# RWKV head sums and norm means as two fp32r passes, with three reorderings around the state chain

## The chip, the cores and the metric

The kernel runs on one core of a Trainium2 chip. The metric is the device time of one execution in microseconds. Five engines share the work: TensorE (PE; its weight loads are shown as PEld), VectorE (DVE), ScalarE (ACT), GpSimd (POOL) and SyncE (SP), which issues the DMAs. All matrix products write to PSUM, from where DVE or ACT take them back.

## The reference, cut to what matters

One decoder layer takes 512 prompt tokens and 8 sequences of 4 sample tokens (544 columns in the kernel, 32 of them samples). It has two branches, an mLSTM and an RWKV-7 branch, which share one input projection, then an output projection and an MLP. The change lies in the RWKV branch alone, which has 16 heads of 64 channels:

```python
kkh = kkh / jnp.maximum(jnp.linalg.norm(kkh, axis=-1, keepdims=True), 1e-12)   # sum over a head
sa = jnp.einsum('bhvk,bhk->bhv', S, -kk)
S = S * w[:, :, None, :] + sa[..., None] * (kk * a)[:, :, None, :] + v[..., None] * k[:, :, None, :]
o = jnp.einsum('bhvk,bhk->bhv', S, r)                                          # token by token
o = head_norm(o, RWKV_NORM_EPS) * lnx_w + lnx_b                                # mean and variance per head
o = o + (rh * kh * r_k).sum(-1, keepdims=True) * vh                            # another head sum
```

## The kernel before

**Layout.** Channels stand on the 128 partitions, tokens along the free axis. Two heads of 64 channels share the partitions, so the RWKV branch is eight "pairs" p = 0 to 7. The 512 prompt tokens are cut in 8 chunks of 64; within a chunk the token recurrence is solved by products, and only the state goes from chunk to chunk.

**Products.** The large projections are done in `mm3` (lines 311 to 316): each fp32 operand is split in a high and a low part of type fp32r, and three fp32r products (L314, L315, L316) replace one fp32 product. A projection of 128 channels is 48 such products (8 blocks of rows, two halves of the columns, three each). The small products of the RWKV branch are plain fp32. In the trace an fp32 product stands as two instructions, an fp32r product as one, and a transpose as one.

**One pair.** `g_proj` (L604) projects k, r and v. `g_prep` (L628) forms the decays and the scaled operands: `heads_sum` (L559) adds the squares of k over each head with the block matrix `bones` (first call at L651), products of `ar` and `bk` (L707) give the masked matrices `g1` and `gk`; `g1` goes through DRAM to be inverted. L750 transposes the `a` half of `ar` by 16 products with the identity into `za` (copied at L751). L756 is the second head sum. L779 transposes v into `sv` (four copies at L783), and L789 multiplies `g1` with it on 64 rows at a time. `g_inv` (L792) solves blocks of 16 rows on DVE (L802, L804), sends the result through DRAM, and completes the inverse by small products. `g_chain` (L855) applies the inverse (L867), forms the transition matrices (L880) and the state input (L889), and goes through the chunks: L899 multiplies the state with the transition matrix, L900 on DVE adds the chunk's input, and two output products per chunk stand in the same loop (L903). L907 adds the part of the output that comes from the state. Then come the head norm's two means, by `bmean` (L912, L919). `g_srows` (L1021) does the same norm for the sample rows (L1026, L1032).

**Order.** Each of these functions is a generator. What it yields is a due time; `merge` (L1041) takes the segment with the smallest base plus due time next, so a due time that has already passed means "at once". That fixes the order of the program. A list scheduler then lays out each engine's queue from the program order and its own estimate of when an operation is ready, so an engine's order can differ from the program's: the trace shows the chain's products between the projections of later pairs. Every queue is worked off in order. Tiles come from pools: `rp` has two buffers for each name, `r1` one, `tp` (PSUM) two, `big()` (PSUM) two.

Of the kernel before, what the change touches and what calls it, by code (L numbers as in the profile page):

```python
# [10 lines left out]
F32 = mybir.dt.float32  # L11
F32R = mybir.dt.float32r
AF = mybir.ActivationFunctionType
ALU = mybir.AluOpType
# [8 lines left out]
NS = NB * NT  # L23
T = NS + NP
# [17 lines left out]
def hybrid_kernel(ctx: ExitStack, tc: tile.TileContext, I, O):  # L42
    nc = tc.nc
    V = nc.vector
    S = nc.scalar
    G = nc.gpsimd
    PE = nc.tensor
# [4 lines left out]
    const = ctx.enter_context(tc.tile_pool(name="const", bufs=1))  # L52
# [12 lines left out]
    def tp(shape):  # L65
        return psB.tile(shape, F32, name="tp")


    ident = const.tile([128, 128], F32)
# [4 lines left out]
    G.memset(onesd, 1.0 / D)  # L74
    bones = const.tile([128, 128], F32)
    G.memset(bones, 0.0)
    G.memset(bones[0:64, 0:64], 1.0)
    G.memset(bones[64:128, 64:128], 1.0)
    bmean = const.tile([128, 128], F32)
    G.memset(bmean, 0.0)  # L80
    G.memset(bmean[0:64, 0:64], 1.0 / 64)
    G.memset(bmean[64:128, 64:128], 1.0 / 64)

# [169 lines left out]
    ps = tp([128, 8, 9])  # L253
# [5 lines left out]
    for k in range(8):  # L259
        ps = big()  # L260
# [5 lines left out]
    ps = tp([128, 128])  # L266
# [23 lines left out]
    nkk = const.tile([128, 8], F32)  # L290
# [242 lines left out]
    with tc.issue_after(mm.ins):  # L533
        ps = proj_w(*xsp, 0, 276, 276, ((0, 6), (6, 8)))
# [5 lines left out]
    r1 = pool(late, "r1", 1, "right")  # L540
# [17 lines left out]

    def heads_sum(mat, src):  # L559
        ps = big()  # L560
        for j, (a, n) in enumerate(HALF):
            PE.matmul(ps[:, j, 0:n], mat, src[:, a:a + n], start=True, stop=True)
        return ps
# [64 lines left out]
    def g_prep(p, s):  # L628
# [21 lines left out]
        S.activation(sq, k_, AF.Square, scale=kkc)  # L650
        ps = heads_sum(bones, sq)  # L651
        S.activation(lw, lw, AF.Copy, scale=CDEC, bias=CDEC)
# [32 lines left out]
        b3, m3 = c8(bp[:, NS:T]), c8(km[:, NS:T])  # L685
        ar = rp.tile([128, 8, 2, 64], F32, name="ar")
        V.scalar_tensor_tensor(ar[:, :, 0, :], k3, nkk[:, p:p + 1], wp[:, :, 0:64], op0=ALU.mult, op1=ALU.mult)
        V.tensor_tensor(ar[:, :, 1, :], r3, wp[:, :, 1:65], op=ALU.mult)
        bk = r1f.tile([128, 8, 3, 64], F32, name="bk")
# [11 lines left out]
        for i, c0 in enumerate((0, 4)):  # L701
            yield 14.83 + 3 * i
            cs = slice(c0, c0 + 4)
            pts = [tp([128, 4, 2, 64]) for h in range(2)]
            for j in range(4):
                for h, q in enumerate(halves):
                    PE.matmul(pts[h][:, j].rearrange("p a b -> p (a b)"),  # L707
                              bk[q, c0 + j, h:h + 2, :].rearrange("p a b -> p (a b)"),
                              ar[q, c0 + j].rearrange("p a b -> p (a b)"), start=True, stop=True)
# [36 lines left out]
        s["za"] = za  # L746
        pt = tp([128, 8, 64])
# [8 lines left out]
        ps = heads_sum(bones, bv)  # L756
        for h, q in enumerate(halves):
# [15 lines left out]

        sv = rp.tile([128, 8, 2, 64], F32, name="sv")
        s["sv"] = sv
        yield 16.44
        pt = tp([128, 4, 128])
        for i in range(4):
            PE.transpose(pt[:, i, :], v_[:, NS + 128 * i:NS + 128 * i + 128], ident)  # L779
        sve = sv.rearrange("p (a e) h v -> p a e h v", e=2)  # L780
        for e, q in enumerate(halves):
            for h in range(2):
                S.copy(sve[halves[1 - h], :, e, h, :], pt[q, :, 64 * h:64 * h + 64])  # L783
        yield 22.9
        pt = tp([128, 8, 64])
        for c in range(8):
            for h, q in enumerate(halves):
                o = halves[1 - h]
                PE.matmul(pt[q, c, :], g1[o, c, h, :], sv[o, c, h, :], start=True, stop=True)  # L789
        S.copy(za[:, :, 1, :], pt)  # L790
# [64 lines left out]
    def g_chain(p, s):  # L855
# [16 lines left out]
        for c0 in (0, 4):  # L872
            yield 59.2 + 0.2 * c0
            j0 = 1 if c0 == 0 else 0
            cs = slice(c0 + j0, c0 + 4)
            n = 4 - j0
            pt = tp([128, 4, 2, 64])
            for j in range(j0, 4):
                for h, q in enumerate(halves):
                    PE.matmul(flat(pt[q, j]), zz[q, c0 + j, :], flat(gk[q, c0 + j, h]), start=True, stop=True)  # L880
            for h, q in enumerate(halves):
                V.tensor_tensor(xmd[q, cs, 64 * h:64 * h + 64], pt[q, j0:4, 1, :],
                                ident[q, q].unsqueeze(1).to_broadcast([64, n, 64]), op=ALU.add)
            V.tensor_tensor(ar[:, cs, 1, :], ar[:, cs, 1, :], pt[:, j0:4, 0, :], op=ALU.add)
        yield 60.6
# [8 lines left out]
        po = psC.tile([128, 8, 64], F32, name="po")  # L894
        for c in range(8):
            yield 61.2 + 1.0 * c
            if c > 0:

                PE.matmul(pcn[:, c, :], xmd[:, c, :], st[:, c - 1, :], start=True, stop=True)  # L899
                V.scalar_tensor_tensor(sc[:, 0:64] if c == 7 else st[:, c, :], pcn[:, c, :], wend[:, c:c + 1],  # L900
                                       st[:, c, :], op0=ALU.mult, op1=ALU.add)
            for h, q in enumerate(halves):
                PE.matmul(po[q, c, :], sv[:, c, h, :], gk[:, c, h, 0, :], start=c == 0, stop=False)  # L903
        yield 68.3
        for c in range(1, 8):
            for h, q in enumerate(halves):
                PE.matmul(po[q, c, :], st[q, c - 1, :], ar[q, c, 1, :], start=False, stop=c == 7)  # L907
# [113 lines left out]
    def g_srows():  # L1021
# [3 lines left out]
        pm = tp([128, 8, NS])  # L1025
        PE.matmul(pm, bmean, o8, start=True, stop=True)  # L1026
        V.tensor_tensor(o8, o8, pm, op=ALU.subtract)
# [3 lines left out]
        pm = tp([128, 8, NS])  # L1031
        PE.matmul(pm, bmean, q8, start=True, stop=True)  # L1032
        S.activation(q8, pm, AF.Sqrt, bias=eps_b)
# [421 lines left out]
    for p in range(8):  # L1455
        st = {}
# [257 lines left out]
```

## Time and profile before

| what | value |
|---|---|
| median of three runs | 1423.55 us (1420.78 to 1434.56) |
| the profiled execution's own time | 1417.81 us |
| its span (first to last instruction) | 1416.1 us |
| PE / PEld / DVE / ACT / POOL busy | 96 / 85 / 59 / 43 / 5% of the span |
| mean granted TensorE clock | 0.985 |

The pairs' work lies between about 100 and 620 us. "Busy" for PE counts an instruction from its start to the end of its pipeline, and neighbouring products overlap, so the time that a product takes from the engine is read from the distance between two starts, not from its duration. A "granted clock" of 1.00 is the full 2.4 GHz and 0.50 is 1.2 GHz.

### The profile page before, as it was taken

The page shows a single profiled execution, that of the slowest core. Times are in us where ns is not written, and L with a number is a line of the kernel's source. Part 1 is how long each engine was busy: PE and PEld are TensorE (multiplying, and loading weights), DVE is VectorE, ACT ScalarE, POOL GpSimd, SP SyncE. Part 2 cuts the span into 40 slices and gives each one's busy share as a digit, 9 for nine tenths or more (in the row PEclk, how much of TensorE's full clock was granted, in tenths as well). Part 3 has the DMA queues.
Part 4 walks back from the last instruction along what each step waited for, and adds up shares of the span by engine and source line. Part 5 has one row for each costly group of instructions (what it writes and reads, how often), then busy time and mean ns, then how long its engine had stood idle before and what let it go on. Part 6 is the DMA issues. An engine that isn't in the chain of part 4 may idle for free.

```text
span 1416.1 us, 29923 instructions
## 1 busy us (share of the span) xinstructions
PE 1363.6 (96%) x12272; PEld 1202.5 (85%) x12272; DVE 831.9 (59%) x2002; ACT 608.0 (43%) x1133; POOL 70.9 (5%) x292
## 2 busy tenths in 40 slices
PE   6999999999999999999999999999999999999996
PEld 3878887888887878888888888678899999999996
DVE  3677575857667686566556465387943343443446
ACT  2465454545545455364454444533741231321320
POOL 6000000000000000011101010000000000000000
PEclk9999999999998999999999999999999999999999
DMA  9432222122222211253655744753513323333321
GB/s 281 126 68 53 67 50 54 46 60 54 60 56 49 69 43 38 57 146 105 204 159 154 243 128 139 237 182 119 149 61 90 90 75 92 88 90 90 103 77 64
DMA packets 251483, 145.66 MB, mean 103 GB/s; under 512 B 52683, under 2 KB 244413, under 8 KB 251323
## 3 DMA queue, kind: packets, MB, share of 16 engines
q1 hardware_dynamic: 251347, 143.75, 35.5%
q8 instruction: 97, 1.59, 0.5%
q14 instruction: 39, 0.32, 0.1%
HBM read 124.58 MB, written 19.14 MB: 101 GB/s over the span
## 4 chain that ended last, share of the span: by engine, by line
PE 77%; DVE 7%; ACT 6%; DMA 5%; issue 3%; SPq 1%; POOL 0%; POOLq 0%; DVEq 0%; ACTq 0%
PE mm L314 17%; PE mm L315 16%; PE mm L316 16%; PE tp L707 2%; DVE wlo L302 1%; DMA craw<-in_w_cond_dram 1%; ACT whi L300 1%; PE tp L340 1%; PE tp L1300 1%; PE pcn L899 1%; PE po L1317 1%; PE tp L880 1%; PE po L903 1%; DMA wraw<-in_w_up_dram 1%; PE tp L867 1%
## 5 line engine op out<-in xcount | busy, mean ns | idle before, releaser
L314 PE MATMUL mm<-hhi,whi 128*128 128x272 f32 (+1 forms) x1712 | 510.6, 299 | 4.1 <-ACT hhi L1529 1.3
L315 PE MATMUL mm<-hlo,whi 128*128 128x272 f32 (+1 forms) x1712 | 502.5, 294 | 0.9 <-DVE hlo L1530 0.8
L316 PE MATMUL mm<-hhi,wlo 128*128 128x272 f32 (+1 forms) x1712 | 500.3, 292 | 0.5 <-DVE wlo L302 0.5
L314 PEld LDWEIGHTS mm<-hhi,whi 128*128 128x128 f32 x1712 | 323.6, 189 | 20.2 <-issue 10.2
L315 PEld LDWEIGHTS mm<-hlo,whi 128*128 128x128 f32 x1712 | 323.6, 189 | 6.6 <-DVE hlo L1530 2.1
L316 PEld LDWEIGHTS mm<-hhi,wlo 128*128 128x128 f32 x1712 | 323.8, 189 | 5.5 <-issue 4.0
L300 ACT CAST whi<-wraw 128x1024 fp32r<-128x1024 f32 (+1 forms) x142 | 146.1, 1029 | 395.4 <-PE mm L315 382.7
L302 DVE TENSOR_TENSOR wlo<-wraw,whi 128x1024 fp32r<-128x1024 f32 (+1 forms) x142 | 170.0, 1198 | 140.0 <-ACT whi L300 137.4
L314 PE MATMUL mm<-hid,whi 128*128 128x272 f32 x384 | 110.8, 289 | 0.0
L316 PE MATMUL mm<-hid,wlo 128*128 128x272 f32 x384 | 110.7, 288 | 0.0
L315 PE MATMUL mm<-hil,whi 128*128 128x272 f32 x384 | 110.4, 288 | 0.0
L314 PEld LDWEIGHTS mm<-hid,whi 128*128 128x128 f32 x384 | 72.3, 188 | 0.5 <-ACT hid L1539 0.5
L315 PEld LDWEIGHTS mm<-hil,whi 128*128 128x128 f32 x384 | 72.3, 188 | 0.0
L316 PEld LDWEIGHTS mm<-hid,wlo 128*128 128x128 f32 x384 | 72.1, 188 | 0.0
L1414 DVE TENSOR_TENSOR g1s<-mm,mod 128x32 f32<-128x32 f32 x48 | 9.1, 190 | 102.3 <-PE mm L316 102.1
L1418 DVE SCALAR_TENSOR_TENSOR xt<-mm,mod,xt 128x240 f32<-128x240 f32 (+2 forms) x92 | 43.6, 476 | 9.3 <-PE mm L316 9.2
L1099 DVE SCALAR_TENSOR_TENSOR acc<-qr,chalf,acc 128x512 f32<-128x512 f32 (+1 forms) x96 | 43.5, 496 | 0.7 <-ACT acc L1097 0.2
L802 DVE TENSOR_TENSOR itmp<-xi,ai 128x2 f32<-128x2 f32 (+14 forms) x120 | 29.8, 248 | 15.4 <-POOL ai L722 12.3
L1539 ACT CAST hid<-rl 128x544 fp32r<-128x544 f32 (+1 forms) x37 | 21.6, 585 | 39.1 <-DVE rl L1538 39.1
L1540 DVE TENSOR_TENSOR hil<-rl,hid 128x544 fp32r<-128x544 f32 (+1 forms) x37 | 23.9, 647 | 19.4 <-ACT hid L1539 19.3
L707 PEld LDWEIGHTS tp<-ar,bk 64*128 64x128 f32 x256 | 25.8, 194 | 9.2 <-issue 6.8
L707 PE MATMUL tp<-ar,bk 64*128 64x128 f32 x256 | 33.1, 304 | 0.5 <-DVE gk L712 0.5
(553 smaller groups left out, 2199.7 us busy)
## 6 DMA issues: line engine op xcount, KB each, us to landing
wraw<-in_w_in_dram SPq DMA_DIRECT2D x66, 512.0 KB
craw<-in_w_cond_dram SPq DMA_DIRECT2D x48, 512.0 KB
wraw<-in_w_up_dram SPq DMA_DIRECT2D x32, 512.0 KB
wraw<-in_w_down_dram SPq DMA_DIRECT2D x32, 512.0 KB
cs<-in_state_mlstm_C_dram SPq DMA_DIRECT2D x32, 256.0 KB
out_C_s_dram<-cs SPq DMA_DIRECT2D x32, 256.0 KB
wraw<-in_w_out_dram SPq DMA_DIRECT2D x12, 384.0 KB
xp<-in_x_prompt_dram SPq DMA_DIRECT2D x2, 2048.0 KB
```

The source lines that it names most:

```text
L300: S.copy(hi, raw)
L302: V.tensor_tensor(lo, raw, hi.bitcast(F32), op=ALU.subtract)
L314: PE.matmul(out, hi[k], xhi[k], start=first and k == 0, stop=False)
L315: PE.matmul(out, hi[k], xlo[k], start=False, stop=False)
L316: PE.matmul(out, lo[k], xhi[k], start=False, stop=last and k == n - 1)
L340: mm = PE.matmul(ps[32 * g:32 * g + 32, i, :], cth[:, 4 * half + g, :], raws[ci][half][:, g, :], start=half == 0, stop=half == 1)
L707: PE.matmul(pts[h][:, j].rearrange("p a b -> p (a b)"), bk[q, c0 + j, h:h + 2, :].rearrange("p a b -> p (a b)"), ar[q, c0 + j].rearrange(" ...
L802: V.tensor_tensor(tmp[:, 0:nq, 0:t + 1], xi[:, 0:nq, 0:t + 1], ai[:, 0:t + 1, t].unsqueeze(1).to_broadcast([128, nq, t + 1]), op=ALU.mult)
L1099: V.scalar_tensor_tensor(a, qr[:, base + j * step:base + j * step + n], w(j), a, op0=ALU.mult, op1=ALU.add)
L1418: V.scalar_tensor_tensor(d, ps[:, o:n], mod[:, goff + m, 0:1], d, op0=ALU.mult, op1=ALU.add)
L1539: S.copy(hid[:, f, a:a + n], rl)
L1540: V.tensor_tensor(hil[:, f, a:a + n], rl, hid[:, f, a:a + n].bitcast(F32), op=ALU.subtract)
```

## The change

It does four things.

1. `bones` and `bmean` become fp32r. Every head sum and every mean is formed by splitting the source in a high part (a copy on ACT) and a low part (a subtraction on DVE), and by two fp32r products that add up in PSUM, in place of one fp32 product. The parts have one buffer each (`shi`, `slo` in `r1`).
2. `ar` is stored with the `a` half and the `r` half apart, and the `a` half is transposed in four 128 by 128 blocks, with four copies on ACT, in place of 16 products with the identity and one copy.
3. `sv` gets zeros in its unused quarters (two GpSimd memsets per pair), moves to a pool with one buffer, and L789 works on all 128 rows.
4. The 16 output products of L903 stand ahead of the chain over chunks, not in it. Two due times change (16.44 to 28, 22.9 to 33); both have passed when they are reached, as the old ones had.

```diff
-    bones = const.tile([128, 128], F32)
+    bones = const.tile([128, 128], F32R)
...
-    def heads_sum(mat, src):
+    def parts_of(src):
+        n = src.shape[1]
+        hi = r1.tile([128, T], F32R, name="shi")[:, 0:n]
+        S.copy(hi, src)
+        lo = r1.tile([128, T], F32R, name="slo")[:, 0:n]
+        V.tensor_tensor(lo, src, hi.bitcast(F32), op=ALU.subtract)
+        return hi, lo
+
+    def sum2(out, mat, hi, lo):
+        PE.matmul(out, mat, hi, start=True, stop=False)
+        PE.matmul(out, mat, lo, start=False, stop=True)
+
+    def heads_sum(src):
+        hi, lo = parts_of(src)
         ps = big()
         for j, (a, n) in enumerate(HALF):
-            PE.matmul(ps[:, j, 0:n], mat, src[:, a:a + n], start=True, stop=True)
+            sum2(ps[:, j, 0:n], bones, hi[:, a:a + n], lo[:, a:a + n])
...
-        ar = rp.tile([128, 8, 2, 64], F32, name="ar")
+        ar = rp.tile([128, 2, 8, 64], F32, name="ar")
...
-        for c in range(8):
-            for q in halves:
-                PE.matmul(pt[q, c, :], ar[q, c, 0, :], ident[q, q], start=True, stop=True)
-        S.copy(za[:, :, 0, :], pt)
+        def swap2(dst, src):
+            pt = tp([128, 4, 128])
+            for i in range(4):
+                PE.transpose(pt[:, i, :], src[:, 128 * i:128 * i + 128], ident)
+            dv = dst.rearrange("p (a e) h v -> p a e h v", e=2)
+            for e, q in enumerate(halves):
+                yield e, q, dv, pt
+        for e, q, dv, pt in swap2(za, ar[:, 0].rearrange("p c t -> p (c t)")):
+            for h, d in enumerate(halves):
+                S.copy(dv[d, :, e, 0, :], pt[q, :, 64 * h:64 * h + 64])
...
-        sv = rp.tile([128, 8, 2, 64], F32, name="sv")
+        sv = r1.tile([128, 8, 2, 64], F32, name="sv")
+        for h, q in enumerate(halves):
+            G.memset(sv[q, :, h, :], 0.0)
...
-                PE.matmul(pt[q, c, :], g1[o, c, h, :], sv[o, c, h, :], start=True, stop=True)
+                PE.matmul(pt[q, c, :], g1[:, c, h, :], sv[:, c, h, :], start=True, stop=True)
...
+        for c in range(8):
+            for h, q in enumerate(halves):
+                PE.matmul(po[q, c, :], sv[:, c, h, :], gk[:, c, h, 0, :], start=c == 0, stop=False)
         for c in range(8):
             yield 61.2 + 1.0 * c
             ...
-            for h, q in enumerate(halves):
-                PE.matmul(po[q, c, :], sv[:, c, h, :], gk[:, c, h, 0, :], start=c == 0, stop=False)
...
-        PE.matmul(pm, bmean, o, start=True, stop=True)
+        sum2(pm, bmean, *parts_of(o))
...
-        PE.matmul(pm, bmean, o2, start=True, stop=True)
+        sum2(pm, bmean, *parts_of(o2))
```

## Rows read from the trace of the kernel before

**Rows 1.** The page's busy times: share of the span and instructions of each engine.

```profile
PE 1363.6 (96%) x12272; PEld 1202.5 (85%) x12272; DVE 831.9 (59%) x2002; ACT 608.0 (43%) x1133; POOL 70.9 (5%) x292
```

**Rows 2.** Busy times by stretch: one pair, then nine stretches' sum over 100 to 620.

```profile
464.20:526.11 61.91, 59.91 (x709) 50.43 (x709) 43.33 (x119) 32.99 (x65) 0.61 (x4) 1.00 0.23 55
...
sum 520.00, PE 508.01 PEld 427.80 DVE 352.05 ACT 267.18 POOL 13.44; mean PE 56.45 PEld 47.53 DVE 39.12 ACT 29.69 POOL 1.49
```

**Rows 3.** PE in order of time, one pair's chain and norm: start, us, operation.

```profile
399.60 0.33 PE L903 MATMUL po<-gk,sv 128*64 128x64 f32 x2
...
402.46 1.15 PE L889 MATMUL tp<-sv,gk 128*64 128x64 f32 x32
403.42 0.55 PE L903 MATMUL po<-gk,sv 128*64 128x64 f32 x10
...
405.92 0.33 PE L899 MATMUL pcn<-st,xmd 128*128 128x64 f32 x2
...
406.77 0.33 PE L899 MATMUL pcn<-st,xmd 128*128 128x64 f32 x2
...
410.77 0.33 PE L899 MATMUL pcn<-st,xmd 128*128 128x64 f32 x2
411.03 0.34 PE L903 MATMUL po<-gk,sv 128*64 128x64 f32 x4
411.29 0.66 PE L961 MATMUL tp<-ident,sl 128*128 128x128 f32 x4
...
413.76 0.34 PE L903 MATMUL po<-gk,sv 128*64 128x64 f32 x4
...
416.50 1.12 PE L912 MATMUL pcn<-o,bmean 128*128 128x512 f32 x2
417.56 1.16 PE L707 MATMUL tp<-ar,bk 64*128 64x128 f32 x12
```

**Rows 4.** The same view, the next transposes, head sum and projection.

```profile
427.72 1.15 PE L750 MATMUL tp<-ident,ar 64*64 64x64 f32 x32
428.80 1.19 PE L562 MATMUL mm<-bv,bones 128*128 128x272 f32 x4
429.62 0.49 PE L314 MATMUL mm<-hhi,whi 128*128 128x276 f32 x1
...
435.93 0.27 PE L770 MATMUL tp<-ident,xv 128*128 128x128 f32 x1
436.04 0.60 PE L779 MATMUL tp<-ident,xv 128*128 128x128 f32 x4
436.57 1.18 PE L556 MATMUL mm<-xwa,w2a 64*128 64x272 f32 x4
```

**Rows 5.** The lines' costs on ACT and DVE: busy, mean ns, idle before.

```profile
L751 ACT COPY za<-tp 128x512 f32<-128x512 f32 x8 | 4.7, 587 | 3.5 <-PE tp L750 3.5
L783 ACT COPY sv<-tp 64x256 f32<-64x256 f32 x32 | 11.7, 367 | 0.8
```

**Rows 6.** Split of 128x544 in the MLP: durations min/median/max on ACT and DVE.

```profile
L1539 ACT CAST hid<-rl x37: 402/647/650, 1013.4 to 1353.9; 128x544 fp32r<-128x544 f32 x27, 128x272 fp32r<-128x272 f32 x10
...
L1540 DVE TENSOR_TENSOR hil<-rl,hid x37: 430/724/727, 1014.0 to 1355.2; 128x544 fp32r<-128x544 f32 x27, 128x272 fp32r<-128x272 f32 x10
```

**Rows 7.** DVE in order of time: masks, inverse, and the way back.

```profile
419.55 0.41 DVE L712 TENSOR_TENSOR gk<-tp,mask 128x256 f32<-128x256 f32 x1
...
428.62 0.16 DVE L802 TENSOR_TENSOR itmp<-xi,ai 128x2 f32<-128x2 f32 x1
...
436.84 0.29 DVE L804 TENSOR_REDUCE xi<-itmp 128x8 f32<-128x128 f32 x1
...
452.42 0.45 DVE L817 STREAM_TRANSPOSE t<-x 128x256 f32<-128x256 f32 x1
```

**Rows 8.** Who waited for whom, 100 to 620: total us, times, longest.

```profile
PEld tp L789 <- ACT sv L783: 8.5, 28, 1.1
```

**Rows 9.** Busy times by stretch: one half-clock stretch.

```profile
440.40:450.70 10.30, 10.30 (x29) 6.60 (x28) 4.92 (x10) 5.76 (x11) 0.07 (x1) 0.50 0.26 56
```

More of the change, by code (lines that the diff above doesn't have):

```diff
@@ L74, in hybrid_kernel @@
     G.memset(onesd, 1.0 / D)
-    bones = const.tile([128, 128], F32)
[L76 to L82, printed above, removed]
+    bones = const.tile([128, 128], F32R)
+    G.memset(bones.bitcast(F32), 0.0)
+    G.memset(bones[0:64, 0:64].bitcast(F32), 1.0)
+    G.memset(bones[64:128, 64:128].bitcast(F32), 1.0)
+    bmean = const.tile([128, 128], F32R)
+    G.memset(bmean.bitcast(F32), 0.0)
+    G.memset(bmean[0:64, 0:64].bitcast(F32), 1.0 / 64)
+    G.memset(bmean[64:128, 64:128].bitcast(F32), 1.0 / 64)
     mask64 = const.tile([128, 128], F32)
@@ L650, in g_prep @@
         S.activation(sq, k_, AF.Square, scale=kkc)
-        ps = heads_sum(bones, sq)
+        ps = heads_sum(sq)
         S.activation(lw, lw, AF.Copy, scale=CDEC, bias=CDEC)
@@ L685, in g_prep @@
         b3, m3 = c8(bp[:, NS:T]), c8(km[:, NS:T])
-        ar = rp.tile([128, 8, 2, 64], F32, name="ar")
-        V.scalar_tensor_tensor(ar[:, :, 0, :], k3, nkk[:, p:p + 1], wp[:, :, 0:64], op0=ALU.mult, op1=ALU.mult)
-        V.tensor_tensor(ar[:, :, 1, :], r3, wp[:, :, 1:65], op=ALU.mult)
+        ar = rp.tile([128, 2, 8, 64], F32, name="ar")
+        V.scalar_tensor_tensor(ar[:, 0], k3, nkk[:, p:p + 1], wp[:, :, 0:64], op0=ALU.mult, op1=ALU.mult)
+        V.tensor_tensor(ar[:, 1], r3, wp[:, :, 1:65], op=ALU.mult)
         bk = r1f.tile([128, 8, 3, 64], F32, name="bk")
@@ L706, in g_prep @@
                 for h, q in enumerate(halves):
-                    PE.matmul(pts[h][:, j].rearrange("p a b -> p (a b)"),
-                              bk[q, c0 + j, h:h + 2, :].rearrange("p a b -> p (a b)"),
-                              ar[q, c0 + j].rearrange("p a b -> p (a b)"), start=True, stop=True)
+                    PE.matmul(pts[h][:, j], bk[q, c0 + j, h:h + 2, :].rearrange("p a b -> p (a b)"),
+                              ar[q, :, c0 + j, :], start=True, stop=True)
             for h in range(2):
@@ L755, in g_prep @@
         V.scalar_tensor_tensor(bv, r_, col("rwkv_r_k", p), km, op0=ALU.mult, op1=ALU.mult)
-        ps = heads_sum(bones, bv)
+        ps = heads_sum(bv)
         for h, q in enumerate(halves):
@@ L772, in g_prep @@
         s["vs_"] = vs_
-        sv = rp.tile([128, 8, 2, 64], F32, name="sv")
+        yield 28
+        sv = r1.tile([128, 8, 2, 64], F32, name="sv")
         s["sv"] = sv
[L776 to L781, printed above, removed]
+        for h, q in enumerate(halves):
+            G.memset(sv[q, :, h, :], 0.0)
+        for e, q, dv, pt in swap2(sv, v_[:, NS:]):
             for h in range(2):
-                S.copy(sve[halves[1 - h], :, e, h, :], pt[q, :, 64 * h:64 * h + 64])
-        yield 22.9
+                S.copy(dv[halves[1 - h], :, e, h, :], pt[q, :, 64 * h:64 * h + 64])
+        yield 33
         pt = tp([128, 8, 64])
@@ L906, in g_chain @@
             for h, q in enumerate(halves):
-                PE.matmul(po[q, c, :], st[q, c - 1, :], ar[q, c, 1, :], start=False, stop=c == 7)
+                PE.matmul(po[q, c, :], st[q, c - 1, :], ar[q, 1, c, :], start=False, stop=c == 7)
         S.copy(o, flat(po))
@@ L1025, in g_srows @@
         pm = tp([128, 8, NS])
-        PE.matmul(pm, bmean, o8, start=True, stop=True)
+        f8 = lambda a: a.rearrange("p a b -> p (a b)")
+        sum2(f8(pm), bmean, *parts_of(f8(o8)))
         V.tensor_tensor(o8, o8, pm, op=ALU.subtract)
@@ L1031, in g_srows @@
         pm = tp([128, 8, NS])
-        PE.matmul(pm, bmean, q8, start=True, stop=True)
+        sum2(f8(pm), bmean, *parts_of(f8(q8)))
         S.activation(q8, pm, AF.Sqrt, bias=eps_b)
```

4 lines of the change are left out of this document (1 added, 3 removed).

## The prediction

> **What bounds the kernel now.** I read the page first: PE is busy 96% of the span, no other engine over 59% [rows 1]. Then the busy times by stretch: over 520 us of pair work PE counts 508.0 us, DVE 352.1, ACT 267.2 [rows 2]. Whether such a busy PE is full is seen in its order of time: a product's cost is the distance from its start to the next start. A whole projection goes through without a break, 48 products in 6.31 us, 0.131 us each [rows 4], and the next operation starts at once. So inside a pair the engine is mostly handed over from product to product, with projections of later pairs as filler, and work taken from PE should shorten the stage. A pair takes some 61.9 us in the stretch shown [rows 2].
>
> A second bound is close by. In DVE's order of time one pair's masks end at 419.96, its inverse starts at 428.62 and ends at 437.13, and the first use of what comes back from DRAM is at 452.42 [rows 7]: 32.5 us in which the pair's own line hangs on two DMA trips and on DVE, whatever PE does. The rest of the period, about 29 us, is small products, copies, the chain over chunks and the next pair's L707, and there PE's order decides.
>
> A third row speaks against taking PE's share as the bound: weight loads fill only 427.8 of the same 520 us, 82% [rows 2]. If that share is the true one, the stage has room on PE, and time taken from it need not come out: rival A, whose price is worked out below from rows. The Trainium skill, "Trainium Kernel Development and Optimization", section Performance Expectations, has this as a rule: matmul busy time is a bad metric for how near a kernel is to its limit, weight-load busy time a good one. By that rule the result would be A's; I keep to the distances between starts, which show no room within a run of products.
>
> **The change, part by part.** The sum is made against the profiled execution, 1417.81 us.
>
> *Head sums.* Two per pair, 16 in all. One is four fp32 instructions, 428.80 to 429.62, 0.82 us [rows 4]. After, four fp32r products of the projection's width: 4 x 0.131 = 0.52. Gain 0.30 x 16 = 4.8 us.
>
> *Norm means.* Two per pair, 16 in all. One takes 416.50 to 417.56, 1.06 us [rows 3]. No fp32r product 512 wide is in the trace; scaled by columns from the 276-wide one, an estimate, it is 0.131 x 512 / 276 = 0.243, two are 0.49. Lower end of the gain zero (no faster than fp32), upper 0.57. I take 0.60 us after, near the scaled row and with a step in or out of another kind of product; gain 0.46 x 16 = 7.4. The two sample means, half as wide, give at most 0.5 together.
>
> *Transposing a.* 32 instructions, 427.72 to 428.80, 1.08 us, become four block transposes like those of v, 436.04 to 436.57, 0.53 us [rows 4]. Gain 0.55 x 8 = 4.4.
>
> *Output products ahead of the chain.* In this pair they stand in six groups, of which three, of four instructions, stand behind chain steps; the first and the last of the six are shown [rows 3]. A group of four takes 411.03 to 411.29, 0.26 us [rows 3]. The same shape in one run (L889) takes 402.46 to 403.42, 0.96 for 32, so four are worth 0.12 [rows 3]. Each group that joins the run saves 0.14: five of six, 8 pairs, 5.6 us. If the engine's queue splits the run as before, zero.
>
> *Products with v on all rows.* Still 32 instructions of 64 columns. The 64-row form took 1.08 us for 32 [rows 4], the 128-row form 0.96 [rows 3]: between zero and 0.1 us per pair. What sets L789 is its wait for the four copies of v, 8.5 us in total [rows 8], and this stays. I count zero. The two memsets go to POOL, which is busy 0.61 us of a pair [rows 2]. Their size has no row; even several us would fit before L789, after `sv`'s last reader in the chain before. `sv` with one buffer is read last by L903 at 413.76 [rows 3] and copied anew after v's transposes at 436.04 [rows 4]: no wait.
>
> *The `ar` layout* only changes strides; zero, as no row shows a stride's price in either direction.
>
> Sum of gains on PE: 4.8 + 7.4 + 0.5 + 4.4 + 5.6 = 22.7 us, 2.8 per pair.
>
> *What is added elsewhere.* Each sum needs a copy on ACT and a subtraction on DVE, 0.65 and 0.72 us for 544 columns [rows 6]. Per pair that is about 4 x 0.65 + 3 extra za copies' worth (4 x 0.367 - 0.587 = 0.88 [rows 5]) = 3.5 us of ACT, and 4 x 0.72 = 2.9 us of DVE. ACT goes from 33.0 to 36.5 and DVE from 43.3 to 46.2 of 61.9 us [rows 2], so neither is full. But the queues are in order. A head sum's result comes some 1.4 us later. For the squares of k the cover is the filler: the masks' products L707 stand behind the chain in PE's queue. If that cover went, 1.4 x 8 = 11 us would be on the path. For the other three sums nobody waits before the next pair. What they can hold up is the inverse, a line of dependent DVE operations from 428.62 to 437.13 [rows 7]: each subtraction that falls within it costs 0.72. Bounds 0 (all outside) and two of them, 1.44 per pair, 11.5 us. I take 0.5 per pair, 4.0 us, because the inverse spans about a seventh of a pair and two of the four sums fall due near it. Behind a subtraction on DVE that waits for ACT's copy stands whatever DVE has next; the one-buffer parts can make two neighbouring sums wait for each other, about 1.4 us, covered by the projection behind them.
>
> Net: 22.7 - 4.0 = 18.7, so 1399 us for an execution like the profiled one. The three runs' median, 1423.55, lies 5.7 above it, so the forecast for the median is 1405 us, 1.3% faster.
>
> **Rivals.**
>
> *A: the line through the DMAs and DVE is the bound, and PE's gain turns into waits.* For it: 32.5 us of 61.9 per pair don't hang on PE [rows 7], and weight loads fill 82% of the time [rows 2]. Then only what lies on the line counts: three groups of output products between chain steps, 3 x 0.26, and one mean between L707's groups, 0.46: 1.24 per pair, 9.9 us; against it one to two subtractions in the inverse, 5.8 to 11.5. Time: 1419 to 1425, no change. Against it: from 406.77 to 410.77 [rows 3] the chain itself stands behind filler for 4 us, so filler that is done earlier gives time back there. Chance 0.25.
>
> *B: the queue keeps the run of output products in pieces* (the change doesn't do what it says; in the program before they also stood elsewhere than on the engine). 5.6 us less: 1410. Chance 0.10.
>
> *C: the chain stands bare.* The output products were what PE did while DVE added a chunk. Two neighbouring steps are 0.85 us apart at the closest shown, 405.92 to 406.77, and a step's own two instructions take 0.26 (410.77 to 411.03) [rows 3]. A bare step leaves PE idle for 0.6 us; seven steps, 4.1 us per pair, against 2.3 that the rest nets: 1.8 x 8 = 14 us slower, 1438, and with the squares' 11 us up to 1449. It decides from four bare steps of seven on. Against it: projections and L961 stand between the steps already [rows 3]. Chance 0.10.
>
> *D: the clock.* One stretch of 10.3 us ran at 0.50 of the clock, 1.2 GHz, right after L789's wait [rows 9]; at 2.4 GHz its work would take about 5 us. Other waits may bring one or two such stretches more: 5 to 10 us, 1410 to 1415; or take them away: 1395 to 1400. Chance of more 0.07, of fewer inside the forecast.
>
> **The numbers.** Forecast 0.48 (own range 1391 to 1412), A 0.25, B 0.10, C 0.10, D 0.07. The best end is 1388: all means at the scaled price, no subtraction inside the inverse, a clock stretch less. The range 1388 to 1424 takes in the forecast, B, D and nearly all of A; C is left out above. One per cent, about what a measurement here can tell from no change, is 14.2 us: under 1409.3 lies most of the forecast and half of B, 0.55; above 1437.8 most of C, 0.10; between them 0.35.
>
> **What would show it.** After, a head sum should stand on PE as four products 0.13 us apart, a mean as two of about 0.25, the transposes of a as four in 0.53, the output products as one run of 32 in about 1 us per pair. Pairs should come 2 to 2.5 us closer. If PE's idle time or the wait of L821 for L817 grows instead, A is right; if the steps of L899 are bare, C. The prediction is wrong if the products shrink as said and the pairs come no closer, or if DVE's inverse grows by more than 1.5 us per pair.

## The result, and the profile after

The changed kernel takes 1436.09 us (median; 1429.55 to 1444.45) where the kernel before takes 1427.23 us in runs beside it: a ratio of 1.0075, 95% interval 1.0051 to 1.0099. It is slower by 9 us, less than one per cent, but with an interval clear of no change. The forecast was 1405 us, the range 1388 to 1424.

The page's line of busy times for the changed kernel, then two stretches of its pair work (start:end, length, busy us of PE, PEld, DVE, ACT, POOL, granted clock, DMA share, GB/s):

```profile
PE 1361.5 (95%) x12048; PEld 1209.5 (84%) x12048; DVE 853.2 (60%) x2036; ACT 632.4 (44%) x1191; POOL 79.1 (6%) x308
...
100.00:620.00 520.00, 492.94 (x5522) 424.01 (x5520) 363.67 (x978) 285.97 (x576) 19.50 (x83) 0.95 0.23 54
523.80:537.40 13.60, 11.28 (x159) 8.84 (x159) 7.29 (x24) 4.94 (x14) 0.00 (x0) 0.50 0.17 49
547.70:561.30 13.60, 13.60 (x75) 11.24 (x72) 5.25 (x12) 5.05 (x11) 0.00 (x0) 0.50 0.07 10
```

Against [rows 1, 2] PE is hardly less busy over the whole program, and in the 520 us of pair work 15 us less busy, yet the span is longer (1432.6 us). So PE's busy time has to be taken apart. I split the time up to the last product in three: **idle**, in which no product's row runs; **half-clock loss**, the busy time times one less the granted clock, summed over the clock's records; and the rest, **work** at full clock. For one execution of each:

| us | work | idle | half-clock loss |
|---|---|---|---|
| before | 1345.3 | 41.7 | 18.3 |
| after | 1327.3 | 60.1 | 34.2 |
| difference | -18.0 | +18.4 | +15.9 |

The 18 us that the change takes from PE are there. Idle time takes them back to the last microsecond, and the half clock comes on top. (The loss column is somewhat too high where much is lost: with the same products, a run below with a loss of 60.9 shows only 1315.7 of work.)

The half-clock loss of one execution is not that of the kernel, so here are all of them. Over 85 executions of the kernel before, taken beside the experiments, the mean granted clock goes from 0.966 to 0.989, and the time falls with it, by some 10 us for each 0.01 (correlation -0.91). The changed kernel's 20 executions have a mean clock of 0.967 where those 85 have 0.978, and on average they lie on the straight line through the others to within 0.5 us. At an equal clock the two kernels take the same time: work and idle cancel, and the 9 us go with the clock (the line gives 11, an estimate).

**Where the idle time is.** The costs by line on PE, 100 to 625 us, in the changed kernel: busy us, mean ns | idle just before, and what ended it.

```profile
L569 PE MATMUL mm<-shi,bones 128*128 128x272 f32 x32 | 10.9, 357 | 3.5 <-ACT shi L563 2.5 <-DVE xr L529 1.0
...
L569 PE MATMUL pcn<-shi,bmean 128*128 128x512 f32 x16 | 7.6, 472 | 2.8 <-ACT shi L563 2.8
...
L764 PE MATMUL tp<-ident,xv 128*128 128x128 f32 x32 | 6.1, 282 | 3.0 <-ACT za L771 3.0
...
L838 PE MATMUL tp<-t,g 32*32 32x32 f32 x512 | 6.0, 193 | 2.8 <-DVE t L834 2.8
L764 PE MATMUL tp<-ident,ar 128*128 128x128 f32 x32 | 5.7, 305 | 2.7 <-ACT gk L755 2.7
...
L947 PE MATMUL pcn<-ident,sc 128*128 128x128 f32 x7 | 2.2, 320 | 2.5 <-ACT lt L940 2.5
```

And the same products in the kernel before (its second execution, run h2 below):

```profile
L562 PE MATMUL mm<-lt,bones 128*128 128x272 f32 x32 | 12.1, 484 | 0.0
L912 PE MATMUL pcn<-o,bmean 128*128 128x512 f32 x16 | 10.8, 762 | 0.0
L562 PE MATMUL mm<-bv,bones 128*128 128x272 f32 x32 | 10.4, 446 | 0.0
L750 PE MATMUL tp<-ident,ar 64*64 64x64 f32 x256 | 9.2, 221 | 0.1
...
L821 PE MATMUL tp<-t,g 32*32 32x32 f32 x512 | 6.0, 193 | 3.0 <-DVE t L817 2.0 <-DVE cw L729 0.7
L779 PE MATMUL tp<-ident,xv 128*128 128x128 f32 x32 | 4.8, 272 | 0.0
L929 PE MATMUL pcn<-ident,sc 128*128 128x128 f32 x8 | 2.5, 314 | 0.0
```

Sums, transposes and the state's transpose wait 14.5 us after and 0.1 us before. PE waits no longer for the line through DRAM and the inverse: L838 2.8 us, where L821 had 3.0. How long that line itself became is a different question, taken up under the period. Idle time in this window grew by 14.6 us, as much as these products carry, while smaller waits come and go; the other 3.8 us lie outside it. How two such waits come about is seen in the changed kernel's order of time (start, us, and in brackets idle before):

```profile
298.29 0.59 ACT L926 COPY o<-po 128x512 f32<-128x512 f32 x1 [4.10 <-PE po L925]
298.91 0.62 ACT L563 CAST shi<-o 128x512 fp32r<-128x512 f32 x1
...
299.58 0.49 PE L569 MATMUL pcn<-shi,bmean 128*128 128x512 f32 x1 [0.47 <-ACT shi L563]
...
307.65 1.50 ACT L771 COPY za<-tp 64x256 f32<-64x256 f32 x4 [0.26 <-PE tp L764]
...
309.20 0.44 PE L764 MATMUL tp<-ident,xv 128*128 128x128 f32 x2 [0.50 <-ACT za L771]
```

The mean's first product comes due behind two ScalarE copies one after the other, where there was one; the transposes of v wait for a bank that four copies of 0.37 us now empty instead of one of 0.59 [rows 5]. What stands ahead of the two in PE's queue is done by then.

**The clock** [rows 9 for a stretch of before]. Ahead of 523.8 us PE was busy 4.59 of 6.8 us, with a wait of 1.8 us for the transposed blocks; ahead of 547.7 it had run 10.30 of 10.30 us without a break, the chain's small products. Both times it fell from 1.00 to 0.50 (2.4 to 1.2 GHz), for 13.6 us. I have no rule from this for when it falls.

**The period** of a pair, first mask (L711, L724) to first mask, did not fall: 60.3 us in the kernel before, 60.6 us after, in the pairs shown, which run at full clock throughout. (The fourth pair took 60.8 and 60.6 us; the third, 58.4 and 60.6, even grew.) These are the kernel before (h2) and the changed kernel, in order of time: masks, read-back `ai`, the transposed blocks, the product that takes them, and the next pair's mask.

```profile
421.15 0.42 DVE L711 TENSOR_TENSOR g<-tp,mask 128x256 f32<-128x256 f32 x1
...
427.19 0.41 DVE L712 TENSOR_TENSOR gk<-tp,mask 128x256 f32<-128x256 f32 x1
...
431.54 1.10 SPq L50 DMA_DIRECT2D ai<-d  x2
...
455.75 0.45 DVE L817 STREAM_TRANSPOSE t<-x 128x256 f32<-128x256 f32 x1
...
456.34 0.74 PE L821 MATMUL tp<-t,g 32*32 32x32 f32 x64
...
481.43 0.42 DVE L711 TENSOR_TENSOR g<-tp,mask 128x256 f32<-128x256 f32 x1
```

```profile
294.78 0.42 DVE L724 TENSOR_TENSOR g<-tp,mask 128x256 f32<-128x256 f32 x1
...
302.15 0.41 DVE L725 TENSOR_TENSOR gk<-tp,mask 128x256 f32<-128x256 f32 x1
...
307.58 1.09 SPq L50 DMA_DIRECT2D ai<-d  x2
...
332.85 0.44 DVE L834 STREAM_TRANSPOSE t<-x 128x256 f32<-128x256 f32 x1
...
333.43 0.74 PE L838 MATMUL tp<-t,g 32*32 32x32 f32 x64
...
355.35 0.42 DVE L724 TENSOR_TENSOR g<-tp,mask 128x256 f32<-128x256 f32 x1
```

Within the period the balance did change. From the first mask to the product that takes the transposed blocks (L821, L838) 35.2 us became 38.7; from there to the next mask 25.1 became 21.9. On the longer part, the read-back is issued 12.8 us after the first mask instead of 10.4, and the inverse takes 10.0 us instead of 8.5. In both kernels the product starts 0.14 us after its blocks are ready, so its short wait on PE doesn't say that the line through DRAM and DVE kept its length: it grew by 3.5 us.

### The profile page after: what moved, and what is told of

Same layout as the page of the kernel before. It is cut to its first block, busy times and chain, and to the rows that moved or that the text cites. A ratio compares the mean times of both kernels' runs of the same rounds, so it can differ in the third digit from the quotient of the medians.

```text
span 1432.6 us, 29642 instructions
## 1 busy us (share of the span) xinstructions
PE 1361.5 (95%) x12048; PEld 1209.5 (84%) x12048; DVE 853.2 (60%) x2036; ACT 632.4 (44%) x1191; POOL 79.1 (6%) x308
## 4 chain that ended last, share of the span: by engine, by line
PE 78%; DMA 7%; ACT 6%; DVE 6%; issue 3%; SPq 1%; POOL 0%; POOLq 0%; DVEq 0%; ACTq 0%
PE mm L314 18%; PE mm L315 17%; PE mm L316 17%; DMA craw<-in_w_cond_dram 3%; DVE wlo L302 2%; PE tp L721 2%; PE tp L1230 1%; ACT whi L300 1%; PE tp L884 1%; PE pcn L919 1%; PE tp L340 1%; PE tp L1242 1%; PE tp L1319 1%; PE po L1336 1%; PE tp L897 1%
## 5 line engine op out<-in xcount | busy, mean ns | idle before, releaser
L721 PE MATMUL tp<-ar,bk 64*128 64x128 f32 x256 | 34.7, 305 | 0.5 <-DVE bk L705 0.3
L721 PEld LDWEIGHTS tp<-ar,bk 64*128 64x128 f32 x256 | 26.1, 195 | 4.9 <-issue 1.8
```

The lines of the kernel that those rows point to most:

```text
L721: PE.matmul(pts[h][:, j], bk[q, c0 + j, h:h + 2, :].rearrange("p a b -> p (a b)"), ar[q, :, c0 + j, :], start=True, stop=True)
```

## The experiments

Ratios are to the kernel before, run beside each; work, idle and loss (us) as above, of the profiled execution. The last column is the mean granted clock over all the executions behind a ratio; the kernel before had 0.981 beside the e runs, 0.979 beside f, 0.978 beside g and 0.976 beside h.

| run | ratio, 95% interval | work | idle | loss | clock |
|---|---|---|---|---|---|
| e1 before, sums issued twice | 1.0129 (1.0111 to 1.0147) | 1367.3 | 38.6 | 19.7 | 0.983 |
| e2 only output products moved | 1.0180 (1.0154 to 1.0206) | 1344.9 | 66.4 | 14.0 | 0.980 |
| e3 only a in full blocks | 1.0031 (0.9994 to 1.0068) | 1339.1 | 45.5 | 38.5 | 0.975 |
| e4 sums, v on all rows | 1.0009 (0.9990 to 1.0028) | 1331.7 | 51.4 | 29.5 | 0.978 |
| f1 after, orders held | 1.0303 (1.0270 to 1.0336) | 1315.7 | 80.7 | 60.9 | 0.949 |
| f2 after, output products back | 1.0096 (1.0064 to 1.0127) | 1331.5 | 59.1 | 36.6 | 0.970 |
| f3 e2, orders held | 1.0261 (1.0228 to 1.0294) | 1344.2 | 71.5 | 36.0 | 0.965 |
| f4 before, orders held | 1.0172 (1.0138 to 1.0206) | 1342.2 | 55.9 | 40.3 | 0.969 |
| g1 after, hi from po | 1.0013 (0.9982 to 1.0044) | 1328.7 | 56.7 | 24.0 | 0.972 |
| g2 after without a's blocks | 1.0065 (1.0032 to 1.0098) | 1326.2 | 55.5 | 46.6 | 0.969 |
| g3 both of these | 0.9953 (0.9924 to 0.9981) | 1329.4 | 50.1 | 26.0 | 0.976 |
| g4 after, sums padded | 1.0008 (0.9979 to 1.0037) | 1344.5 | 52.1 | 16.0 | 0.982 |
| h1 after again | one execution, 1439.9 us | 1326.9 | 60.8 | 39.5 | 0.968 |
| h2 before again | one execution, 1429.7 us | 1344.5 | 43.0 | 29.7 | 0.976 |
| h3 g3, one wait less | 0.9978 (0.9947 to 1.0009) | 1328.0 | 52.1 | 39.3 | 0.972 |
| h4 e4, hi from po | 1.0117 (1.0055 to 1.0179) | 1336.6 | 53.2 | 47.6 | 0.966 |

### More work on PE, and each part alone

```diff
# e1, on the kernel before (the means likewise)
-            PE.matmul(ps[:, j, 0:n], mat, src[:, a:a + n], start=True, stop=True)
+            for _ in range(2):
+                PE.matmul(ps[:, j, 0:n], mat, src[:, a:a + n], start=True, stop=True)
```

e2, e3 and e4 are the diff's own parts on the kernel before; the due times of the step that copies v stay 16.44 and 22.9 in all of them, and the sums go with v's edit because the room that `sv` gives up is what their parts stand in.

> The kernel before, with every fp32 head-sum and mean product of a pair issued twice (the first result is overwritten by the second). PE gets 2 x 0.82 + 2 x 1.06 = 3.8 us more per pair, 30 us in all. Theory L (a pair's period is the line through the two DRAM trips, the inverse on DVE and the chain): only the mean between the masks' products lies on that line, about 1 us per pair, 8 us; most likely 0 to 10 us slower, ratio 1.000 to 1.007, and a pair's period at full clock stays within 1 us of the 60.3 us of before. Theory P (PE's work sets the period): 30 us slower, ratio 1.021, periods 3 to 4 us longer.

> The kernel before, with the output products in one run ahead of the chain and nothing else of the change. Theory L: in the queue of the DMA issues the read-back of the blocks to be inverted still follows its write directly, so the first DRAM trip stays at some 8.5 us; the run costs about 0.8 us ahead of the chain and saves about as much in it: period 59.5 to 61 us, ratio 0.996 to 1.004. Theory P: 5.6 us faster, ratio 0.996. A bare chain would show as steps of the state products that are idle on PE for 0.6 us, ratio above 1.01.

> The kernel before, with a transposed in full blocks (the new layout of ar with it) and nothing else of the change. Theory L: no more than queue order matters; two of the pairs get the load of g2 and a weight block ahead of the read-back, 2 us each: ratio 0.998 to 1.004. Theory P: 4.4 us faster, ratio 0.997.

> The kernel before, with the head sums and means as two fp32r passes and, since the parts need its room, v's tile with one buffer and its products on all rows; the chain and the transposes of a are as before. Theory L: PE's 12 us go into waits, the subtractions on DVE add up to 1.4 us per pair to the inverse, and one or two pairs have loads ahead of the read-back: 0 to 10 us slower, ratio 1.000 to 1.007. Theory P: 12 us faster, ratio 0.991. Theory C (less PE work brings more half-clock stretches): periods at full clock unchanged, more stretches at 0.50.

By their ratios, theory L is met in e3 and e4, theory P in none; e1 lies between the two, e2 far above both. In e1 the period rises from 60.3 to 62.9 us: the kernel before has hardly any idle PE to give, and work added there costs nearly its length. In e3 the reverse shows for once: late pairs at full clock take 59.6 and 59.0 us, work is 6.2 us less, idle only 3.8 us more. The profiled execution, one of the longest of ten, also lost 20 us more to the half clock; over all ten the clock is lower by 0.006, some 6 us on the line above, so no gain is left. In e4 work falls by 13.6, idle rises by 9.7. Only e2 costs by itself, and at hardly a lower clock. There PE waits where it had not:

```profile
L314 PE MATMUL mm<-hhi,whi 128*128 128x276 f32 (+1 forms) x543 | 165.2, 304 | 14.9 <-DVE xk L529 9.8 <-DVE xi L804 3.3 <-DVE cw L729 1.8
...
L562 PE MATMUL mm<-bv,bones 128*128 128x272 f32 x32 | 11.0, 466 | 8.0 <-DVE ggs L946 8.0
L821 PE MATMUL tp<-t,g 32*32 32x32 f32 x512 | 6.0, 194 | 9.9 <-DVE t L817 9.9
```

All three wait for DVE, whose queue in a steady pair of this program has 25 other instructions inside the inverse (2 in the kernel before, 6 in the changed one); the inverse takes 19.7 us. The scheduler had laid out all queues anew for a move of 16 products per pair. That made me suspect the orders.

### Holding the orders (f1 to f4)

```diff
# f1, on the changed kernel; f4 the same on the kernel before; f3 on e2, without the two DMA lines
+    def behind(k):
+        return tc.issue_after(LAST[k]) if k in LAST else ExitStack()
...
-            dma(raw, view)
-            return split(raw, pool)
+            with behind("ai"):        # last read-back of ai
+                dma(raw, view)
+            with behind("inv"):       # last step of the inverse
+                return split(raw, pool)
...     # g2's load behind "ai"; xv's mix and the sums' subtraction behind "inv"
# f2, on the changed kernel
         for c in range(8):
-            for h, q in enumerate(halves):
-                PE.matmul(po[q, c, :], sv[:, c, h, :], gk[:, c, h, 0, :], start=c == 0, stop=False)
-        for c in range(8):
             yield 61.2 + 1.0 * c
```

(f2 puts the loop over h back at the end of the step, as before.)

> The changed kernel with nothing but queue orders altered: on VectorE the weight splits, the xv mix and the low parts of the sums are held behind the last step of the inverse of the pair traced last; on SyncE's queue the weight blocks and the g2 block are held behind the read-back of ai. No instruction is added or removed. In the changed kernel the read-back's issue begins 3.3 us after the end of the write's issue (1.2 us in the kernel before) and the inverse takes 10.0 us (8.5 us) with six other VectorE instructions inside it. ORDER (the pair's period is a line through two DRAM trips, the inverse and the chain, and the static orders set its length): the line gets 2 us shorter at the read-back and 1.5 to 2 us at the inverse, period 60.6 us to 56.5 to 57.5 us, seven pairs, so 21 to 28 us less than the changed kernel: 1408 to 1415 us, ratio to the kernel before 0.986 to 0.992. PE WORK (the products' own time sets the period): nothing taken from TensorE, 1434 to 1438 us, ratio 1.005 to 1.010. CLOCK (the loss is the half-clock stretches): the same stretches as in the changed kernel, some 50 us of half clock, 1430 us or more. Risk for ORDER: weights that come later leave TensorE waiting at the projections.

> The changed kernel with the output products put back between the chain's steps; all its other edits stay. The orders then settle otherwise: in a steady pair four other VectorE instructions inside the inverse instead of six, and the read-back directly behind the write on SyncE's queue, as in the kernel before. ORDER: the period returns to that of the kernel before, 58 to 60 us, 1418 to 1426 us, ratio 0.996 to 1.003. PE WORK: the output products cost 0.7 us per pair more, eight pairs, 1436 + 6 = 1442 us, ratio 1.012. CLOCK: half-clock time as in the changed kernel, 1432 us or more.

> The kernel before with the output products alone moved ahead of the chain, as in the run that took 1444 us at a period of 64.9 us, and now the xv mix and the weight splits held behind the inverse on VectorE: in a steady pair eight other VectorE instructions stand inside the inverse instead of 25. ORDER (that run lost its time to an inverse of 18.9 us): the inverse falls to 9 to 11 us, the period to 58 to 60 us, 1410 to 1425 us, ratio 0.993 to 1.003. MOVED PRODUCTS THEMSELVES (the loss is PE's: 32 products in one block ahead of the chain, queued before something that the chain needs): no change, 1440 to 1448 us, ratio 1.014 to 1.02.

> Control: the kernel before with the same holding of queue orders as in the changed kernel with altered orders (VectorE: weight splits and xv mix behind the inverse; SyncE: weight blocks and g2 behind the read-back). In its steady pairs the read-back already stands directly behind the write; the inverse gets six other instructions inside it instead of two. ORDER: nothing won at the read-back, up to 1 us lost at the inverse: period 57 to 60 us, 1416 to 1430 us, ratio 0.997 to 1.007. PE WORK: no change, 1418 to 1423 us.

The theory ORDER falls in the form in which I had put it: all four were off, f1 by more than 50 us and in sign. PE WORK in f1 and f4 and MOVED PRODUCTS in f3 missed as well. The inverse did get shorter in f1, 7.8 us, but the split weights come later, and the projections wait for them:

```profile
L321 PE MATMUL mm<-hhi,whi 128*128 128x276 f32 (+1 forms) x484 | 148.8, 307 | 12.9 <-ACT whi L300 12.9
L323 PE MATMUL mm<-hhi,wlo 128*128 128x276 f32 (+1 forms) x483 | 146.1, 303 | 13.6 <-DVE wlo L302 13.6
```

So a shorter inverse did not bring the period down here, but f1 put another wait in its place and can't tell whether the line through DRAM sets the period of the changed kernel. f4 has the computation of the kernel before and loses 1.7% to the orders alone: 14 us of idle, 22 us of half clock. f2 shows that the moved output products aren't what the changed kernel loses by.

### The waits themselves (g1 to g4)

```diff
# g1, on the changed kernel
+        hi = r1.tile([128, T], F32R, name="shi")[:, 0:NP]
+        S.copy(hi, flat(po))
+        lo = r1.tile([128, T], F32R, name="slo")[:, 0:NP]
+        V.tensor_tensor(lo, flat(po), hi.bitcast(F32), op=ALU.subtract)
         S.copy(o, flat(po))
...
-        sum2(pm, bmean, *parts_of(o))
+        sum2(pm, bmean, hi, lo)
# g4, on the changed kernel, in sum2
+        for _ in range(3):
+            PE.matmul(out, mat, hi, start=True, stop=True)
         PE.matmul(out, mat, hi, start=True, stop=False)
```

g2 is the changed kernel with the old transposing of a, the old layout of `ar`, and v's old due times; g3 is g2 with g1's edit.

> The changed kernel, but the high and low parts of o for its mean are made straight from the sum's bank (po) and o itself is copied out behind them, so that the mean's first product no longer waits for two ScalarE copies one behind the other. In the changed kernel that product (L569) stood idle 0.46 us per pair for the second copy, the v transposes 0.50 us and the a transposes 0.37 us for ScalarE's copies, all told 2.3 us of idle TensorE per pair against 0.7 us in the kernel before. OWN WAITS (what the products saved came back as waits for ScalarE steps that the change itself adds): idle falls by 0.4 to 0.5 us per pair, 3 to 4 us of 1436: 1430 to 1434 us, ratio 1.003 to 1.007. CLOCK (the loss is half-clock time, 14 to 16 us more than in the kernel before): no change, 1434 to 1440 us. PE WORK as forecast (products set the period and idle is noise): 1436 us.

> The changed kernel without the transposes of a in full blocks (a is brought round as in the kernel before, in 32 products and one copy; the layout of ar is the old one); sums, v on all rows and the output products ahead of the chain stay. OWN WAITS: the v transposes no longer wait 0.50 us for four copies of za, nor the a products 0.37 us; 0.6 us per pair of products comes back; net 0 to -0.3 us per pair, 1433 to 1437 us, ratio 1.004 to 1.007. PE WORK: plus 0.55 us per pair, 1440 us, ratio 1.010.

> Both of the two: the changed kernel without the transposes of a in full blocks, and with the parts of o made straight from po. Its queue orders settle as in the kernel before (the read-back directly behind the write; three other VectorE instructions inside the inverse). OWN WAITS: idle per pair falls from 2.3 us to about 1.0 to 1.4 us, products 0.55 us longer: net -0.4 to -0.8 us per pair, 1428 to 1433 us, ratio 1.001 to 1.005. CLOCK: 1434 us or more. PE WORK: 1440 us.

> The changed kernel with three further products of the high part ahead of each head sum and mean (their output is overwritten): about 2.9 us of TensorE per pair, 23 us in all, more than the four-pass products took in the kernel before; the two waits per sum and the ScalarE and VectorE steps stay. Its queue orders settle as in the kernel before (three other VectorE instructions inside the inverse, read-back behind the write). PE WORK: 1436 + 23 = 1459 us, ratio 1.022. OWN WAITS: the new products stand behind the same waits and cannot fill them: idle stays at 2.3 us or so, 1450 to 1459 us. CLOCK (fewer products, more half clock): 10 to 15 us of half-clock loss is won back, 1440 to 1448 us.

g4 is the plainest answer: three products more per sum, 17.2 us in all by the split or 2.2 per pair, and the kernel is faster than the changed one (ratio 1.0008 against 1.0075). The period goes up by 0.75 us only (61.3 against 60.6 in a pair of each), and half-clock loss is less than half (16.0 against 34.2; the clock over all executions 0.982 against 0.967):

```profile
100.00:620.00 520.00, 505.09 (x5727) 441.22 (x5728) 372.07 (x987) 293.46 (x586) 19.31 (x84) 0.99 0.23 56
```

Neither OWN WAITS (1450 or more) nor PE WORK (1459) had that; CLOCK had the direction, and 1428.5 us is below even its range. PE WORK is dead for the changed kernel: idle fell by 8.0 us, so its PE had room for about half of what was added. In e1 idle fell by 3.1 for 22.0 of work. g1 came out at its expected end and better; the wait of the mean is mostly gone (0.6 us), idle 3.4 us less, loss 10 us less. g2 alone gives nothing: idle falls by 4.6 us, loss rises by 12. g3 is 0.5% faster than the kernel before, the only version that is, and better than any of its three theories had it. Its remaining waits on PE:

```profile
L569 PE MATMUL mm<-shi,bones 128*128 128x272 f32 x32 | 10.6, 349 | 2.1 <-ACT shi L563 2.1
L764 PE MATMUL tp<-ident,ar 64*64 64x64 f32 x256 | 10.0, 233 | 2.7 <-ACT gk L756 2.7
...
L949 PE MATMUL pcn<-ident,sc 128*128 128x128 f32 x8 | 2.5, 314 | 2.5 <-ACT lt L942 2.5
```

g1 and g3 also settle into other queue orders than the changed kernel (read-back directly behind the write, three or four instructions in the inverse), so their gain is not the wait alone. Set on the line of time against clock, g1 lies 2.6 us and g3 6.3 us under the kernel before; of the 9 us that g1 wins over the changed kernel by the ratios, some 6 go with the clock.

### Repeats, one wait more, and order at equal work (h1 to h4)

```diff
# h3, on g3
-        pt = psC.tile([128, 128], F32, name="pcn")
+        pt = psC.tile([128, 128], F32, name="po")
         PE.transpose(pt, s["sc"], ident)
```

h4 is e4 with g1's edit.

> The changed kernel as it is, a second profiled execution. In the first, TensorE's busy time was 1361.5 us of which 34.2 us were lost to the half clock (busy time times one less the granted clock, summed), 60.1 us were idle, and 1327.3 us were work at full clock; in the kernel before 18.3, 41.7 and 1345.3 us. OWN WAITS: idle and full-clock work repeat within 2 us. CLOCK AS A PROPERTY OF THE KERNEL: the loss repeats, 28 to 40 us, with stretches at the same places. CLOCK BY CHANCE: the loss differs by over 8 us, and the time with it.

> The kernel before as it is, a second profiled execution. OWN WAITS: idle 41 to 43 us and 1344 to 1347 us of work at full clock again. CLOCK AS A PROPERTY OF THE KERNEL: 15 to 22 us lost to the half clock again. CLOCK BY CHANCE: a loss as large as in the changed kernel's first execution (28 us or more) can come here too.

> The version that was 0.5 per cent faster than the kernel before (the changed kernel without the transposes of a in full blocks, the parts of o made straight from po), and the transpose of the state sc now goes into po's bank instead of pcn's. That product (L949 there) stood idle 0.42 us per pair until ScalarE had read pcn's bank. OWN WAITS: 0.4 us per pair less idle, seven pairs, 3 us: 1417 to 1420 us where the kernel before is at 1427, ratio 0.992 to 0.995. If the wait only moves to the next product: no change, ratio 0.995 to 0.997. Its steady pairs have five other VectorE instructions inside the inverse instead of three, which may take the gain back.

> The two-pass sums and v on all rows alone (output products and a as in the kernel before), as in the run that took 1.0009 times the kernel before, and the parts of o made straight from po. In that run the mean's first product hardly waited (idle under 0.15 us), so this edit takes no wait away; but the queue orders settle in the other way: g2's load and a weight block stand ahead of the read-back on SyncE, and six other VectorE instructions inside the inverse, as in the changed kernel. ORDER (the way in which the orders settle costs time by itself): 1.5 to 2 us per pair, 8 to 14 us: ratio 1.007 to 1.011. OWN WAITS: ratio 0.998 to 1.003, the same as without the edit.

Work and idle repeat within 1.3 us in both kernels. The changed kernel's loss repeats (34.2, 39.5), its pair stretches mostly at the same places; these are from its second execution:

```profile
523.80:537.40 13.60, 11.21 (x158) 8.77 (x159) 7.35 (x24) 4.94 (x14) 0.00 (x0) 0.50 0.18 52
547.70:561.30 13.60, 13.60 (x74) 11.18 (x71) 5.29 (x12) 5.00 (x10) 0.00 (x0) 0.50 0.08 11
```

That of the kernel before does not (18.3, 29.7). So between these executions the half clock costs the change some 5 to 21 us, 13 between the means, in part by chance (11 by the line through all executions); idle costs it 18 every time. In h3 L949's wait is gone and the next product has it:

```profile
L804 PE MATMUL tp<-sv,g 128*64 128x64 f32 x256 | 16.7, 239 | 7.0 <-ACT sv L799 5.9
```

In g3 L949 waited 2.5 us and L804 as long, 0.6 of it for `sv`. No gain, as the expectation's second case said. h4 against e4, near the same work, but orders that settle as in the changed kernel: 1.1% slower, work 4.9 and idle 1.8 us more, loss 18 us more in the profiled executions. Order does cost, then, and in part by way of the clock: over all executions h4's clock is 0.010 under that of the kernel before beside it, some 10 of its 17 us on the line. What the rest is, these runs don't show.

## Why the prediction was wrong

**The step that failed** is the first: "work taken from PE should shorten the stage", read off distances between starts that show no room. They show that PE has no room now, and e1 confirms it (2.6 us of period for 2.8 us of work). They don't show how far the next limit is. It was close: of e3's 6.2 us 3.8 came back as idle time, of e4's 13.6 9.7, of the change's 18.0 all, and the period stayed at 60.6 us against 60.3. PE now stands before products that wait for ScalarE. An addition of 2.2 us per pair to the changed kernel costs 0.75 us of period (g4). On top comes the half clock, with which the 9 us of the result go.

**The sum of PE's gains** was 22.7 us; work fell by 17.6 to 18.0. Undisturbed, a mean takes 0.46 us (0.60 taken), four transposes of a 0.50 (0.53 taken), a head sum about 0.6 (0.52 taken: its first product is 0.2 behind another operation). The output products stand as 2, 8 and 22 and save 0.48 us per pair, not 0.70. Together the sizes came out 5 us short of the sum, which alone would have left a gain.

**What was added elsewhere**: "neither is full", "nobody waits before the next pair", "covered by the projection behind them". This is where idle time shows. Whether these copies set the period, or the longer line below would have kept it anyway, is not shown. The three further copies of za were priced at 0.88 us of ScalarE and left off the path, though they hold a PSUM bank that the next transposes need; the hi copy was priced as ScalarE time though it stands between o and the mean. A projection behind a waiting product covers nothing, as PE's queue is in order; only one ahead of it does.

**The inverse** was charged 0.5 us per pair; it grew by 1.5 (8.5 to 10.0), the mark I had set for being wrong. Together with the later read-back it makes up the 3.5 us by which the way to L838 grew.

**The rivals.** A had the outcome, PE's gain turned into waits, and by the prediction's own sign, more idle time on PE, it would be right; but that sign does not tell its line from ScalarE's copies. For A is that the line grew by 3.5 us while the rest shrank by 3.2. Against it is g4, where the way from first mask to the product is back at 35.4 us and the period still 61.3. f1, with its late weights, decides nothing. So A's mechanism is neither shown nor out. Its 32.5 us "whatever PE does" were misread in any case: that pair holds the half-clock stretch of [rows 9]. In the pair at full clock above, last mask to L817 takes 28.2 us (30.3 after), 4.3 us less, so the line hangs on PE's clock as well. Nor does the chain stand behind filler from 406.77 to 410.77, as was said against A: a step at 407.55 lies between. The rule that stood behind A in the prediction (the Trainium skill, "Trainium Kernel Development and Optimization", Performance Expectations) fits in that PE's 95% told nothing; but weight loads, 82% of the 520 us before and after, told no more. A's 1419 to 1425 lacks D's clock, which was priced at 5 to 10 us with a chance of 0.07 and cost about 11 by all executions (13 in the profiled ones). C is out: the steps are about 1.0 us apart with L721 and L925 between them, and the chain takes 7.0 us where it took 9.0. One chance does not add up: under 1409.3 the parts named give 0.48 and 0.05, not 0.55.

**Open**: what sets the changed kernel's period, the copies or the line through DRAM; what makes the half clock fall where it does; and how much of g1's and g3's gain is the wait and how much the order that came with it. In the runs at hand, the three whose orders settle as in the changed kernel (it, g2, h4) lose 34 to 48 us to the clock, those that settle as before (before, e4, g1, g3, g4) 16 to 30; e3, f2 and h3, with 39, 37 and 39, don't fit. Over all executions the first three have the lowest clocks of these kernels, 0.966 to 0.969, the others 0.970 to 0.982.

## What to carry to other kernels

A busy engine without gaps says that added work costs; to price work taken away, go through the products in the engine's queue and ask of each what it would wait for if it came up earlier. Count a copy that empties a bank, or that stands between a result and its use, as path and not as load of an idle engine. Compare kernels by many executions, with the clock of each beside its time. And where a scheduler lays out the queues, test an edit in several neighbouring forms: here the order alone moved the same computation by 1 to 2%.

## What the runs showed of the hardware

Time follows the granted clock: over 85 executions of one kernel, with mean clocks from 0.966 to 0.989, it falls by some 10 us in 1425 for each 0.01 that the clock is higher. In the changed kernel's pair work seven of eight falls of the clock begin at the same microsecond in two executions (523.8 and 547.7 us among them, 13.6 us each), so there they belong to what the program does; in the kernel before one of three comes at the same place of the program. And a kernel with 17 us more of products ran 0.7% faster by its ratios, with a mean granted clock of 0.982 against 0.967.
